# Decoder trunk on one core: the constants' table and two small tiles padded to multiples of 64 bytes

## The chip, the cores and the metric

The kernel runs on one core of a Trainium2 chip. The metric is the device time of one execution in microseconds; the kernel before is given as the median of three runs.

## The reference

A decoder trunk of two layers on 256 tokens of width 2048, all float32. Layer 0 mixes tokens with a Mamba-2 SSD mixer, layer 1 with forgetting attention (FoX):

```python
for i in range(DEPTH):
    hn = rmsnorm(h, norm_mix_pre[i])
    mix = ssd_mixer(hn, ...) if i % 2 == 0 else fox_mixer(hn, ...)
    h = h + rmsnorm(mix, norm_mix_post[i])
    ff = swiglu(rmsnorm(h, norm_ffn_pre[i]), ffn_w_gate[i], ffn_w_up[i], ffn_w_down[i])
    h = h + rmsnorm(ff, norm_ffn_post[i])
    pe = rmsnorm(p[i] @ ple_w_proj[i], ple_norm[i])
    h = h + jax.nn.sigmoid(h @ ple_w_gate[i]) * pe
```

Nearly all of the arithmetic is in the weight products: `ssd_in`, `ssd_out`, `fox_in`, `fox_out`, and for each layer gate, up (2048 to 5632), down (5632 to 2048), the gate of the per-layer input and its small projection. Their weights are some 500 MB, and each is read once.

## The kernel before

**Units and stages.** Activations lie with features on the partitions and the 256 tokens along the row. A weight product is cut into *units* of 2 to 6 blocks of 128 output features (`unit`, L196). A unit walks through its weights in *stages* of at most 1024 columns: `emit_stage` loads a stage from memory into a tile `raw`, ACT casts it to `wh` (L173, the part that fits fp32r), and DVE subtracts to get the rest, `wl` (L175). Activations are kept in the same two parts side by side: a tile of 512 columns, `x[:, 0, :]` high and `x[:, 1, :]` low. For each block and each 128 input features TensorE then runs a *pair*: a 512-column matmul of both parts against `wh` (L232) and a 256-column one of the high part against `wl` (L234). The weights are the stationary operand (each matmul has its own weight load) and the activations the moving one.

Two kinds of units differ. The last unit of some products (`sep`) runs three matmuls of 256 columns (L227 to L229) instead of a pair. The five token-major units of FoX (`tok`, L221 to L223) make the activations stationary and stream 412 or 416 columns of `wh` or `wl`.

**Which activations are in which tile.** `x`: ssd_in, the front half of ssd_out, gate, up, fox_out and the per-layer gate (5008 pairs, 384 `sep` matmuls). `xq`: the back half of ssd_out. `a`: the input of down. `xb`: the input of FoX. `psp`: the two tiles of the small projection, whose matmuls (L371 to L375, 256 columns each, same weight tiles) fill the time around a norm.

**Who decides the places.** Tiles come from pools that are laid one after another in each partition's memory, each tile at the next multiple of 32 bytes. The first pool, `cp`, begins with `vec`, a table of per-feature constants of `_NV` = 466 columns of 4 bytes, 1864 bytes. Everything up to the last tile of that pool, then the pools of weights, `h`, `x` and `ev`, follow behind it. `ev` holds `ms` and `rs`, the two-column statistics that `rstd_small` makes for a norm, 8 bytes each in slots of 32. The pools behind `ev` that hold `a`, `xq` and `xb` follow its end. The pool of `psp` is laid from the other end of the memory.

The built programs of before and of the change give these byte addresses within a partition (all buffers of a name share the remainder):

| Tile | First address before | mod 64 | mod 128 | First address after | mod 64 | mod 128 |
|---|---|---|---|---|---|---|
| wh | 43552 | 32 | 32 | 43584 | 0 | 64 |
| wl | 59936 | 32 | 32 | 59968 | 0 | 64 |
| x | 92704 | 32 | 32 | 92736 | 0 | 64 |
| a, xq, xb | 137920 | 0 | 64 | 138112 | 0 | 0 |
| psp | 225248 | 32 | 96 | 225248 | 32 | 96 |

Pieces inside a tile (a block of 128 weights is 512 bytes, half an activation tile 1024) keep these remainders. In the token-major units the second piece of a stage lies 1648 (412 columns) or 1664 bytes (416) behind the first.

Of the kernel before, what the change touches and what calls it, by code (L numbers as in the profile page):

```python
# [14 lines left out]
P = 128  # L15
# [29 lines left out]
_NV = 0  # L45
for _n, _w in (
# [4 lines left out]
    ("dt_bias", 1), ("a_log", 1),  # L51
):
    _VEC[_n] = _NV
    _NV += _w


def tile_trunk(ctx, tc, a, out):
# [17 lines left out]
    def nm(s):  # L75
        cnt[0] += 1
        return f"{s}_{cnt[0]}"
# [169 lines left out]
    def tmp(tag, shape=(P, T), dt=F32, bufs=2):  # L247
        return ev.tile(list(shape), dt, tag=tag, name=nm(tag), bufs=bufs)

    def misc():  # L250
        return psm.tile([P, 512], F32, tag="mi", name=nm("mi"))
# [24 lines left out]
    def rstd_small(acc, n):  # L276
        ps = misc()
        for j in range(2):
            PE.matmul(ps[:, j * P:(j + 1) * P], lhsT=acc[:, j * P:(j + 1) * P], rhs=ones,
                      start=True, stop=True)  # L280
        ms = tmp("ms", (P, 2))
        for j in range(2):
            dmark[0] = V.tensor_scalar(out=ms[:, j:j + 1], in0=ps[:, j * P:j * P + 1], scalar1=1.0 / n,  # L283
                                       scalar2=EPS, op0=mult, op1=add)
        rs = tmp("rs", (P, 2), bufs=3)
        G.tensor_tensor(out=rs, in0=ms, in1=mhalf, op=ALU.pow)  # L286
        return rs

# [91 lines left out]
    def post_norm(fill):  # L380
        for f in fill[:FILL_A]:
            f()
        rs = rstd_small(ssb, D)
        for _ in range(PRE_A):
            emit_stage(mark[0], dmark[0])
        for f in fill[FILL_A:FILL_B]:
            f()
        rstd_wide(rs, rwide)
        for _ in range(PRE_B):
            emit_stage(mark[0], dmark[0])  # L390
        for f in fill[FILL_B:]:
            f()
# [39 lines left out]
    def mk_r(half=True, small=None):  # L432
        r = []

        def f1():
            r.append(rstd_small(ssb, D))
            if small is not None:
                V.tensor_copy(out=small, in_=r[0])

        def f2():  # L440
            rstd_wide(r[0], rwide)
            if half:
                V.tensor_scalar(out=rwide2, in0=rwide, scalar1=0.5, scalar2=None, op0=mult)
        return f1, f2
# [19 lines left out]
    def tail(i, mpx, m, pp, mk_next):  # L464
# [63 lines left out]
        def mkpe():  # L528
            rs = rstd_small(ssp, D)
            rstd_wide(rs, rpe)  # L530
            V.tensor_scalar(out=rpe, in0=rpe, scalar1=0.5, scalar2=None, op0=mult)
# [561 lines left out]
```

## Time and profile before

| | |
|---|---|
| Median of three runs | 2813.49 us (2811.70 to 2813.92) |
| Span of the profiled execution, first to last instruction | 2811.0 us |
| TensorE busy | 2782.5 us, 99% of the span |
| VectorE (DVE) busy | 1927.1 us, 69% |
| ScalarE (ACT) busy | 1484.4 us, 53% |

The profiled execution has no time of its own beside its span; the span stands 2.5 us under the median of the three runs. In the rows below, a group of TensorE instructions is named by its line and tiles: `acc<-x,wh` is a matmul that writes `acc` with activations from `x` and weights from `wh`. Matmuls overlap, so the duration of one (some 0.39 us for 512 columns) is longer than the distance from its start to the next one's start; what a matmul costs in a full pipeline is that distance.

### The profile page before, as it was taken

How to read it: one execution, taken by the hardware profiler on the slowest of the kernel's cores; microseconds unless marked ns; L12 is line 12 of the kernel's file. 1: busy time of each engine (PE TensorE's matmuls, PEld its weight loads, DVE VectorE, ACT ScalarE, POOL GpSimd, SP SyncE). 2: the span in 40 equal slices, each digit the busy share in tenths (PEclk: the TensorE clock that was granted, in tenths of full speed). 3: DMA queues.
4: the chain of work that ended last, by engine and by line, in shares of the span. 5: the costliest groups of instructions: out<-in, count | busy, mean ns of one | idle time of the engine just before them, and what ended most of it. 6: DMA issues, size and time to landing. Idle time of an engine off the chain costs nothing.

```text
span 2811.0 us, 43190 instructions
## 1 busy us (share of the span) xinstructions
PE 2782.5 (99%) x16306; PEld 2439.5 (87%) x16306; DVE 1927.1 (69%) x3033; ACT 1484.4 (53%) x2455; POOL 182.8 (7%) x235
## 2 busy tenths in 40 slices
PE   9999999999999999999999999999999999999999
PEld 8888888889788888888897998888888888888888
DVE  8888888855966645666669556766866545666577
ACT  6586676544654444445446544555654444445454
POOL 2000000000300000000005000000200000000022
PEclk9999999999999999999999999999999999999999
DMA  7666665565566656666555676645666656656545
GB/s 234 189 196 184 190 191 173 159 201 180 158 201 188 188 192 189 187 177 192 195 169 166 184 209 191 177 161 164 180 189 188 194 188 185 192 171 204 193 153 176
DMA packets 262512, 520.09 MB, mean 185 GB/s; under 512 B 17392, under 2 KB 42128, under 8 KB 262304
## 3 DMA queue, kind: packets, MB, share of 16 engines
q1 hardware_dynamic: 258640, 504.96, 58.5%
q0 software_dynamic: 3520, 12.15, 1.4%
q8 instruction: 127, 2.08, 0.3%
q14 instruction: 81, 0.66, 0.1%
q10 hardware_dynamic: 144, 0.24, 0.0%
HBM read 515.10 MB, written 2.18 MB: 184 GB/s over the span
## 4 chain that ended last, share of the span: by engine, by line
PE 91%; DVE 4%; issue 3%; ACT 1%; POOL 0%; DMA 0%; DVEq 0%; ACTq 0%; POOLq 0%
PE acc L232 53%; PE acc L234 27%; PE acc L229 1%; PE acc L227 1%; PE acc L228 1%; PE acc L222 1%; PE acc L223 1%; PE acc L221 1%; DVE x L264 1%; PE mi L748 1%; DVE wl L175 1%; DVE sg L411 1%; ACT wh L173 0%; DVE x L261 0%; DVE h L419 0%
## 5 line engine op out<-in xcount | busy, mean ns | idle before, releaser
L232 PE MATMUL acc<-x,wh 128*128 128x512 f32 x5008 | 1730.7, 398 | 12.5 <-DVE x L264 6.7
L175 DVE TENSOR_TENSOR wl<-raw,wh 128x1024 fp32r<-128x1024 f32 (+4 forms) x1020 | 1182.9, 1165 | 793.4 <-ACT wh L173 790.4
L173 ACT CAST wh<-raw 128x1024 fp32r<-128x1024 f32 (+4 forms) x1020 | 1006.4, 993 | 1003.0 <-PE acc L232 825.2
L234 PE MATMUL acc<-x,wl 128*128 128x256 f32 x5008 | 1331.8, 281 | 7.0 <-DVE wl L175 6.8
L232 PEld LDWEIGHTS acc<-x,wh 128*128 128x128 f32 x5008 | 928.1, 188 | 226.0 <-DVE x L264 14.5
L234 PEld LDWEIGHTS acc<-x,wl 128*128 128x128 f32 x5008 | 932.1, 189 | 32.9 <-DVE wl L175 10.5
L232 PE MATMUL acc<-a,wh 128*128 128x512 f32 x1232 | 425.2, 392 | 0.0
L234 PE MATMUL acc<-a,wl 128*128 128x256 f32 x1232 | 339.2, 280 | 0.0
L232 PEld LDWEIGHTS acc<-a,wh 128*128 128x128 f32 x1232 | 229.9, 188 | 49.1
L234 PEld LDWEIGHTS acc<-a,wl 128*128 128x128 f32 x1232 | 231.4, 188 | 2.2
L232 PE MATMUL acc<-xb,wh 128*128 128x512 f32 x512 | 181.9, 398 | 0.0
L255 ACT COPY tb<-acc 128x256 f32<-128x256 f32 (+1 forms) x401 | 139.2, 369 | 38.5 <-PE acc L234 19.6
L234 PE MATMUL acc<-xb,wl 128*128 128x256 f32 x512 | 144.8, 283 | 0.0
L286 POOL TENSOR_TENSOR rs<-ms,mhalf 128x2 f32<-128x2 f32 x18 | 21.2, 1177 | 1764.5 <-DVE ms L283 1764.5
L232 PEld LDWEIGHTS acc<-xb,wh 128*128 128x128 f32 x512 | 95.9, 188 | 20.0
L234 PEld LDWEIGHTS acc<-xb,wl 128*128 128x128 f32 x512 | 96.4, 188 | 0.8 <-issue 0.2
L256 DVE TENSOR_TENSOR g<-acc,tb 128x256 f32<-128x256 f32 x204 | 78.6, 415 | 2.1 <-ACT tb L255 1.5
L232 PE MATMUL acc<-xq,wh 128*128 128x512 f32 x224 | 77.6, 392 | 0.0
L730 ACT ACTIVATE E<-ab,bias 128x128 f32<-128x128 f32 x192 | 59.7, 390 | 15.7 <-PE mi L750 14.8
L658 DVE SCALAR_TENSOR_TENSOR g<-xr,vec,g 128x256 f32<-128x256 f32 x144 | 62.5, 477 | 4.2 <-ACT g L655 3.8
L234 PE MATMUL acc<-xq,wl 128*128 128x256 f32 x224 | 62.3, 280 | 0.0
L273 POOL TENSOR_TENSOR ssb<-ssb,sqp 128x256 f32<-128x256 f32 x60 | 55.6, 927 | 61.9 <-ACT sqp L272 57.5
(209 smaller groups left out, 2305.9 us busy)
## 6 DMA issues: line engine op xcount, KB each, us to landing
raw<-down SPq DMA_DIRECT2D x176, 512.0 KB, 4.1
raw<-ssd_in SPq DMA_DIRECT2D x152, 512.0 KB, 4.6
raw<-gate SPq DMA_DIRECT2D x128, 512.0 KB, 4.3
raw<-up SPq DMA_DIRECT2D x128, 512.0 KB, 4.5
raw<-fox_in SPq DMA_DIRECT2D x64, 512.0 KB, 4.0
raw<-gate SPq DMA_DIRECT2D x64, 384.0 KB, 3.4
raw<-up SPq DMA_DIRECT2D x64, 384.0 KB, 3.7
raw<-ssd_out SPq DMA_DIRECT2D x40, 512.0 KB, 3.7
```

The lines of the kernel that those rows point to most:

```text
L173: A.copy(out=wh[:, :kc * n], in_=raw[:, :kc * n])
L175: V.tensor_tensor(out=wl[:, :kc * n], in0=raw[:, :kc * n], in1=wh.bitcast(F32)[:, :kc * n], op=sub)
L221: PE.matmul(o, lhsT=xh, rhs=wh[:, c, :], start=st, stop=False)
L222: PE.matmul(o, lhsT=xh, rhs=wl[:, c, :], start=False, stop=False)
L223: PE.matmul(o, lhsT=x[:, 1, t * P:(t + 1) * P], rhs=wh[:, c, :], start=False, stop=sp)
L232: PE.matmul(accs[t], lhsT=wh[:, c, t * P:(t + 1) * P], rhs=x.rearrange("p a n -> p (a n)"), start=st, stop=False)
L234: PE.matmul(accs[t][:, :T], lhsT=wl[:, c, t * P:(t + 1) * P], rhs=x[:, 0, :], start=False, stop=sp)
L255: A.copy(out=tb[:np_], in_=acc[:np_, T:2 * T])
L256: V.tensor_tensor(out=o, in0=acc[:np_, :T], in1=tb[:np_], op=add)
L273: (eng or V).tensor_tensor(out=acc, in0=acc, in1=sq, op=add)
L658: V.scalar_tensor_tensor(out=c, in0=xr[:, k:k + T], scalar=col(f"conv_w{k}", cc), in1=c, op0=mult, op1=add)
L730: A.activation(E[:, i, b * P:(b + 1) * P], ab[:, i, lo:lo + P], AF.Relu, scale=-1.0, bias=bias3[:, b, h0 + i:h0 + i + 1])
```

## The change

`_NV` is rounded up to a multiple of 16 columns, from 466 to 480 (1920 bytes), so all that lies behind `vec` moves by 32 bytes. `ms` and `rs` get 16 columns instead of 2, of which the first two are used, so their five slots take 64 bytes each instead of 32, and what lies behind them moves by 192 bytes in all. Every engine has the same instructions in the same order as before; the one that differs in size is the load of `vec`, 480 columns instead of 466.

```diff
@@ -52,6 +52,7 @@
 ):
     _VEC[_n] = _NV
     _NV += _w
+_NV = -(-_NV // 16) * 16
...
@@ -278,11 +279,11 @@
...
-        ms = tmp("ms", (P, 2))
+        ms = tmp("ms", (P, 16))[:, :2]
...
-        rs = tmp("rs", (P, 2), bufs=3)
+        rs = tmp("rs", (P, 16), bufs=3)[:, :2]
```

## Rows read from the trace of the kernel before

**Rows 1.** Page, parts 1 and 2: busy time of engines; granted TensorE clock by slice.

```profile
PE 2782.5 (99%) x16306; PEld 2439.5 (87%) x16306; DVE 1927.1 (69%) x3033; ACT 1484.4 (53%) x2455; POOL 182.8 (7%) x235
...
PEclk9999999999999999999999999999999999999999
```

**Rows 2.** Page, part 4: the chain that ended last, by engine.

```profile
PE 91%; DVE 4%; issue 3%; ACT 1%; POOL 0%; DMA 0%; DVEq 0%; ACTq 0%; POOLq 0%
```

**Rows 3.** Whole run, TensorE groups with shapes: count | busy us, mean ns | idle before.

```profile
L232 PE MATMUL acc<-x,wh 128*128 128x512 f32 x5008 | 1730.7, 398 | 12.5 <-DVE x L264 6.7 <-DVE x L261 2.4 <-ACT wh L173 0.8
L234 PE MATMUL acc<-x,wl 128*128 128x256 f32 x5008 | 1331.8, 281 | 7.0 <-DVE wl L175 6.8
L232 PE MATMUL acc<-a,wh 128*128 128x512 f32 x1232 | 425.2, 392 | 0.0
L234 PE MATMUL acc<-a,wl 128*128 128x256 f32 x1232 | 339.2, 280 | 0.0
...
L232 PE MATMUL acc<-xq,wh 128*128 128x512 f32 x224 | 77.6, 392 | 0.0
L234 PE MATMUL acc<-xq,wl 128*128 128x256 f32 x224 | 62.3, 280 | 0.0
...
L228 PE MATMUL acc<-a,wh 128*128 128x256 f32 x176 | 49.1, 280 | 0.0
...
L227 PE MATMUL acc<-x,wh 128*128 128x256 f32 x128 | 36.2, 283 | 0.0
...
L374 PE MATMUL acc<-psp,wh 128*128 128x256 f32 x64 | 17.8, 278 | 0.0
```

**Rows 4.** Timeline of TensorE, a stretch of units on x: start us, duration us.

```profile
881.09 0.39 PE L232 MATMUL acc<-x,wh 128*128 128x512 f32 x1
881.32 0.27 PE L234 MATMUL acc<-x,wl 128*128 128x256 f32 x1
...
897.73 0.39 PE L232 MATMUL acc<-x,wh 128*128 128x512 f32 x1
```

**Rows 5.** Timeline of TensorE, a later stretch of units on x.

```profile
903.33 0.40 PE L232 MATMUL acc<-x,wh 128*128 128x512 f32 x1
...
911.81 0.40 PE L232 MATMUL acc<-x,wh 128*128 128x512 f32 x1
```

**Rows 6.** Timeline of TensorE, a stretch of units on a.

```profile
1004.93 0.39 PE L232 MATMUL acc<-a,wh 128*128 128x512 f32 x1
...
1021.57 0.39 PE L232 MATMUL acc<-a,wh 128*128 128x512 f32 x1
```

**Rows 7.** Timeline of TensorE, a stretch of units on xb.

```profile
1683.26 0.39 PE L232 MATMUL acc<-xb,wh 128*128 128x512 f32 x1
...
1693.66 0.39 PE L232 MATMUL acc<-xb,wh 128*128 128x512 f32 x1
```

**Rows 8.** Timeline of TensorE, the filler matmuls on psp.

```profile
707.42 0.28 PE L371 MATMUL acc<-psp,wh 128*128 128x256 f32 x1
...
709.12 0.28 PE L371 MATMUL acc<-psp,wh 128*128 128x256 f32 x1
```

**Rows 9.** TensorE groups from 1085 to 1326 us (gate and up units alone).

```profile
L232 PE MATMUL acc<-x,wh 128*128 128x512 f32 x689 | 235.2, 395 | 0.0
L234 PE MATMUL acc<-x,wl 128*128 128x256 f32 x688 | 182.8, 279 | 0.0
```

**Rows 10.** Whole run, TensorE groups of the token-major units, 416 columns wide.

```profile
L223 PE MATMUL acc<-wh,xb 128*128 128x416 f32 x32 | 11.3, 352 | 0.0
L221 PE MATMUL acc<-wh,xb 128*128 128x416 f32 x32 | 11.3, 352 | 0.0
L222 PE MATMUL acc<-wl,xb 128*128 128x416 f32 x32 | 11.2, 349 | 0.0
```

**Rows 11.** Page, part 5: the weight split on DVE and ACT.

```profile
L175 DVE TENSOR_TENSOR wl<-raw,wh 128x1024 fp32r<-128x1024 f32 (+4 forms) x1020 | 1182.9, 1165 | 793.4 <-ACT wh L173 790.4
L173 ACT CAST wh<-raw 128x1024 fp32r<-128x1024 f32 (+4 forms) x1020 | 1006.4, 993 | 1003.0 <-PE acc L232 825.2
```

## The prediction

> **What bounds the kernel now.** I read the page's busy times first: TensorE is busy 99% of the span, and its clock is granted in full, 2.4 GHz, in every slice [rows 1]. The chain that ended last says the same: 91% of it is TensorE [rows 2]. So the question is not who waits but how far apart TensorE's instructions start. The engines that make the weights ready are no second limit. A stage of 1024 columns is eight pairs, some 2.8 us of TensorE; DVE takes 1.17 us for it and ACT 0.99, and DVE stood idle 793 us before this work and ACT 1003 us, ACT mostly until TensorE had freed a buffer [rows 11]. If pairs get a per cent faster, these two follow.
>
> Next, the distance from start to start. In a stretch of units on `a`, 48 pairs lie between the first row and the last: 16.64 us, 346.7 ns a pair [rows 6]. On `xb` 30 pairs take 10.40 us, again 346.7 [rows 7]. On `x` there are two rhythms: in one stretch 48 pairs take 16.64 us, 346.7 each [rows 4]; in a later one 24 pairs take 8.48 us, 353.3 each [rows 5]. The columns alone would take (512 + 256) / 2.4 = 320 ns, so a pair pays 27 or 33 ns on top. The same shapes, the same weight tiles, the same clock; what differs is the activation tile. By the table of places `x` begins 32 bytes past a multiple of 64 (all sixteen buffers), and `a`, `xq` and `xb` on one.
>
> The groups give means. The trace's durations overlap, but a constant ties them to the distances: on `a` the two durations add up to 392 + 280 = 672 ns [rows 3] against a distance of 346.7, so 162.7 ns each. Over the whole run `x` has 398 + 281 = 679 ns, 7 more than `a`; `xq`, aligned like `a`, has its 672 [rows 3]. Part of the 7 are waits: 12.5 + 7.0 = 19.5 us stand as idle before these groups [rows 3], 3.9 ns per pair. The rest is 3.1 ns, between the two rhythms. From 1085 to 1326 us, without any wait, `x` has 395 + 279 = 674, 2 more than `a` [rows 9]. In the three-matmul units a 256-column matmul has 283 ns on `x` and 280 on `a` [rows 3].
>
> **The change part by part.** No instruction is added, removed or moved. The wider load of `vec` is 14 columns more of 466 in one early transfer, and the padding of `ms` and `rs` costs only memory: I take both at nothing: the load is 7 KB more beside some 500 MB of weights that take the whole 2811 us, which uncovered would be 0.04 us.
>
> *Pairs on x.* Their activations come to a multiple of 64, where `a`, `xq` and `xb` lie today without ever showing the slower rhythm in rows 6 and 7. I take the price that leaves out the waits: 3.1 ns x 5008 = 15.5 us off the path. Bounds: 2 ns (the clean stretch, rows 9) gives 10 us; 7 ns (all of the difference, waits included) gives 35 us; nothing at all is a rival below.
>
> *Three-matmul units on x.* 283 to 280 ns, 3 ns x 384 = 1.2 us, bounds 0 and, at the same price for those on `a` and `xq` too, 3 us.
>
> *Token-major units.* Here the weights stream. With 412 columns the first of a stage's two pieces goes from 32 to 0 mod 64, the second from 16 to 48; with 416 both go from 32 to 0. At 3 ns, as above, the pieces that reach 0 (192 + 96 matmuls) give 0.9 us; the others I leave. Bounds: 0 and 1.4 us, or as much lost should 48 be worse than 16.
>
> *The weights as stationary operand.* All blocks of `wh` and `wl` go from 32 to 0 mod 64, for some 15,000 matmuls. No unit of today has both operands aligned, so this needs two ends. The token-major units hold aligned stationary tiles (`xb`, 0 mod 64) under misaligned moving ones: (352 + 352 + 349) / 3 = 351 ns [rows 10], less 162.7 is 188.3, 15 ns over 416 / 2.4 = 173.3. A 512-column matmul on `a`, with misaligned weights, has 392 - 162.7 - 213.3 = 16 ns over, a 256-column one 10.6. Aligned weights buy nothing visible there: end one, 0 us. The other end is the fastest matmul of the trace: the filler on `psp` starts 15 matmuls in 1.70 us, 113.3 ns each [rows 8], 4 ns under the 280 - 162.7 = 117.3 of `a`. If aligned weights brought every matmul there, 15,000 x 4 ns = 60 us. I take 0, since the filler's own weights are misaligned today and can't owe their speed to this.
>
> *Sum.* 15.5 + 1.2 + 0.9 = 17.6 us. The profiled span is 2811.0 us, so 2793.4; the span is 2.5 us under the median of the runs, so the forecast is 2796 us. What the pairs save is not taken back by the 19.5 us of waits on DVE and ACT unless all of those scale, and a per cent of 19.5 us is 0.2. The likeliest case's own range is 2790 to 2803.
>
> **The rivals.**
>
> *The place isn't what sorts the tiles: no change, 2811 to 2815 us.* `x` also lies lower in memory than `a`, `xq` and `xb`, and `x` stays where it is but for 32 bytes. For it: in part of its stretches `x` runs at 346.7 ns, misaligned as it is [rows 4], and `psp`, at 32 mod 64 too, has the fastest matmuls of all [rows 8]. Against it: in a stretch of 48 pairs twelve of the sixteen tiles, over 24 KB, take their turn without a change of rhythm [rows 4], and `a`, `xq` and `xb` agree with each other across both layers [rows 3, 6, 7].
> The Trainium skill gives this rival a reason: "SBUF — State Buffer", in its section "Door 1: The DMA port swizzle", puts the memory's lines at 16 bytes, so a tile at a multiple of 32 already begins on a line, and by that rule the padding buys nothing and the time stays at 2813. Rows 4 and 5 against rows 6 show a difference that this line size doesn't explain.
>
> *Aligned weights pay as well: 2736 to 2796 us*, the term above between its ends, 2766 in the middle. For it: every matmul still pays 10 to 16 ns over its columns, and the filler shows that 6.6 is possible. Against it: the token-major rows.
>
> *What counts is the distance between moving and stationary operand, mod 128: 2795 to 2804 us, but from other units.* The distances today are 0 for `x`, 32 for `a`, 64 for `psp`, and the 256-column matmuls take 120.3, 117.3 and 113.3 ns in that order. After the change `x` keeps 0 and `a`, `xq`, `xb` get 64. At the filler's best, 4 ns x (2 x 1968 + 624) = 18 us; at its mean of 278 ns [rows 3], 2 ns, 9 us.
>
> *Slower: equal remainders mod 64 collide.* If what makes `x` slow is that its blocks and those of `wh` sit at the same remainder, `x` stays slow (0 and 0) and the 1968 pairs on `a`, `xq` and `xb` join it: 3.1 ns x 1968 + 3 ns x 624 = 8 us, at the slow rhythm throughout 6.6 x 1968 + 1.9 = 15 us; 2821 to 2828. It decides from 2.9 ns a pair on, 0.2% of the run. Against it: `psp` and `wh` share 32 today and are fastest; the token-major units don't share, and pay 15 ns.
> By the Trainium skill, "TensorE: Matmul & The Clock Gate", the part "Step-by-step: what each phase is for", the moving operand and the weight load have read ports of their own and don't take from each other, so neither of these last two should exist. No row here shows the ports.
>
> **How the numbers follow.** Likeliest case 0.47; weights too 0.18; distance mod 128 0.12; no change 0.14; slower 0.09. Within 0.2% (5.6 us) of before is about what this measurement can't tell from no change. Faster: 0.47 + 0.18 + 0.12 = 0.77, of which I move 0.01 to the same for the weakest of the third. The range 2765 to 2815 holds the likeliest case, the distance case, no change, and half of the weights' case: 0.47 + 0.12 + 0.14 + 0.09 = 0.82.
>
> **What the profile after would show.** Right: `acc<-x,wh` and `acc<-x,wl` together at 672 to 676 ns in the whole-run groups, no stretch of `x` at 353 ns a pair, `acc<-a` unchanged at 392 and 280, the three-matmul units on `x` at 280. If the weights matter, `acc<-a` falls below 392 and 280 too. If it is the distance, `a` falls and `x` stays at 398 and 281. If remainders collide, `a` rises to `x`. If `x` and `a` both stay, the place wasn't it. The forecast fails most simply if aligned `x` has its own second rhythm.

## The result, and the profile after

The changed kernel takes 2818.99 us (median of ten runs, 2818.04 to 2820.79) against 2812.61 for the kernel before (ten runs, 2811.70 to 2813.92): the ratio is 1.0024 [1.0014, 1.0033], slower by 6.4 us and outside the predicted range. The interval lies wholly above 1, though it reaches down past the 0.2% that was named as the limit. The profiled execution spans 2817.1 us, 6.1 more than before.

In the page after (busy us, share, count; granted clock by slice; chain by engine) what has grown is TensorE's time, by 6.5 us (its weight loads, which overlap with it, by 2.3, and POOL, busy for 7% of the span, by 2.1): VectorE and ScalarE are within 1 us of before [rows 1, 2], and the clock is full.

```profile
PE 2789.0 (99%) x16306; PEld 2441.8 (87%) x16306; DVE 1926.4 (68%) x3033; ACT 1485.2 (53%) x2455; POOL 184.9 (7%) x235
...
PEclk9999999999999999999999999999999999999999
...
PE 90%; DVE 4%; issue 4%; ACT 1%; DMA 1%; POOL 0%; DVEq 0%; ACTq 0%; POOLq 0%
```

The TensorE groups of the whole run after (count | busy us, mean ns | idle before; line numbers are one higher than before):

```profile
L233 PE MATMUL acc<-x,wh 128*128 128x512 f32 x5008 | 1729.4, 398 | 12.4 <-DVE x L265 6.2 <-DVE x L262 2.6 <-ACT wh L174 1.0
L235 PE MATMUL acc<-x,wl 128*128 128x256 f32 x5008 | 1331.5, 281 | 6.7 <-DVE wl L176 6.6
L233 PE MATMUL acc<-a,wh 128*128 128x512 f32 x1232 | 429.8, 394 | 0.0
L235 PE MATMUL acc<-a,wl 128*128 128x256 f32 x1232 | 340.9, 281 | 0.0
L233 PE MATMUL acc<-xb,wh 128*128 128x512 f32 x512 | 184.4, 401 | 0.0
L235 PE MATMUL acc<-xb,wl 128*128 128x256 f32 x512 | 145.8, 285 | 0.0
L233 PE MATMUL acc<-xq,wh 128*128 128x512 f32 x224 | 78.4, 394 | 0.0
L235 PE MATMUL acc<-xq,wl 128*128 128x256 f32 x224 | 62.6, 281 | 0.0
...
L228 PE MATMUL acc<-x,wh 128*128 128x256 f32 x128 | 36.2, 283 | 0.0
...
L375 PE MATMUL acc<-psp,wh 128*128 128x256 f32 x64 | 17.9, 280 | 0.0
```

The group of `xb` in the same view of before:

```profile
L232 PE MATMUL acc<-xb,wh 128*128 128x512 f32 x512 | 181.9, 398 | 0.0
L234 PE MATMUL acc<-xb,wl 128*128 128x256 f32 x512 | 144.8, 283 | 0.0
```

Set beside [rows 3]: `x`, the group that should have gained, has the same 398, 281 and 283 ns. `a` and `xq`, which should have stayed, went from 392 and 280 to 394 and 281, `xb` from 398 and 283 to 401 and 285, and `psp` from 278 to 280. The stretch of gate and up units alone says the same of `x`, 395 and 279 ns as in [rows 9] (TensorE groups, 1085 to 1326 us, after):

```profile
L233 PE MATMUL acc<-x,wh 128*128 128x512 f32 x684 | 233.4, 395 | 0.0
L235 PE MATMUL acc<-x,wl 128*128 128x256 f32 x684 | 181.7, 279 | 0.0
```

And a stretch of units on `a` now shows the rhythm that only `x` had. TensorE's timeline after (start us, duration us):

```profile
1007.11 0.39 PE L233 MATMUL acc<-a,wh 128*128 128x512 f32 x1
...
1023.71 0.40 PE L233 MATMUL acc<-a,wh 128*128 128x512 f32 x1
```

47 pairs lie between the two rows: 16.60 us, 353.2 ns each, where [rows 6] gave 346.7. Not every stretch on `a` is that slow: over the whole run its pairs now average 350.7 ns.

To see where all of the time went I took from each trace every matmul's start to the next one's start, less its columns / 2.4, called that the "excess", and summed it by tile, where both matmuls belong to the six groups below; what is more than 40 ns over counts as a wait. The columns take 2421.0 us, all other matmuls and gaps about 111 us and waits at the other tiles some 7 us in the two kernels and in the variants tabled below, so these sums are what differs:

```
excess in us    x      a      xb     xq    token-major  psp   waits at x   first to last matmul
before        151.5   38.7   13.0   7.0      8.4        1.6      45.9           2805.7
after         150.6   43.6   15.4   7.8      7.4        1.9      45.8           2811.8
```

`a` +4.9, `xb` +2.4, `xq` +0.8, `psp` +0.3, `x` -0.9, token-major -1.0: +6.5 us against 6.1 measured. The loss is found, and nearly all of it is in the tiles that the prediction left alone.

### The profile page after: what moved, and what is told of

It is laid out like the page before. It is cut to its first block, busy times and chain, and to the rows that moved or that the text cites. A ratio compares the mean times of both kernels' runs of the same rounds, so it can differ in the third digit from the quotient of the medians.

```text
span 2817.1 us, 43190 instructions
## 1 busy us (share of the span) xinstructions
PE 2789.0 (99%) x16306; PEld 2441.8 (87%) x16306; DVE 1926.4 (68%) x3033; ACT 1485.2 (53%) x2455; POOL 184.9 (7%) x235
## 4 chain that ended last, share of the span: by engine, by line
PE 90%; DVE 4%; issue 4%; ACT 1%; DMA 1%; POOL 0%; DVEq 0%; ACTq 0%; POOLq 0%
PE acc L233 53%; PE acc L235 27%; PE acc L229 1%; PE acc L228 1%; PE acc L230 1%; PE acc L224 1%; PE acc L223 1%; PE acc L222 1%; DVE wl L176 1%; DVE x L265 1%; PE mi L749 1%; DVE sg L412 1%; DVE x L262 0%; DVE h L420 0%; ACT wh L174 0%
## 5 line engine op out<-in xcount | busy, mean ns | idle before, releaser
L235 PEld LDWEIGHTS acc<-x,wl 128*128 128x128 f32 x5008 | 931.6, 189 | 33.0 <-DVE wl L176 10.7
```

The source lines that it names most:

```text
L235: PE.matmul(accs[t][:, :T], lhsT=wl[:, c, t * P:(t + 1) * P], rhs=x[:, 0, :], start=False, stop=sp)
```

## The experiments

What the addresses suggested after the result: not where a tile lies counts, but how far the activations lie from the weights that TensorE holds. Taken modulo 256 bytes (activation address less weight address, from the built programs), `x` was at 0 and stays at 0, since table padding moves both; `a`, `xq` and `xb` went from 160 to 64, since 160 bytes of padded statistics tiles lie between them and the weights; `psp` went from 192 to 160. The main rival was the prediction's own, that equal remainders mod 64 collide.

**The two halves of the change.** One kernel has only the wider table, one only the wider statistics tiles.

```diff
 # table alone
+_NV += 14
 # statistics tiles alone
-        ms = tmp("ms", (P, 2))
+        ms = tmp("ms", (P, 16))[:, :2]
-        rs = tmp("rs", (P, 2), bufs=3)
+        rs = tmp("rs", (P, 16), bufs=3)[:, :2]
```

> Only the table is padded: weights, x and a all move by 32 bytes together, psp stays. Distance theory (what counts is the address of the moving tile minus that of the weights, mod 256): the distances stay 0 for x and 160 for a, xq and xb, so a stays at 346.7 ns a pair and the time at that of before, 2811 to 2815 us; only psp goes from 192 to 160 and its matmuls from about 113 to about 117 ns. Own-place theory (what counts is where a tile itself lies, and weights at a multiple of 64 cost): the weights are now at 64 mod 128, as in the change, so a goes to 349 to 353 ns a pair and the time to 2818 to 2821 us.

> Only the two statistics tiles are padded: a, xq and xb move by 160 bytes, weights and x stay. Distance theory: a, xq and xb are now 64 from the weights, as in the change, so a is at 349 to 353 ns a pair and the time at 2817 to 2821 us, the whole loss. Own-place theory with the weights as the cause: the weights have not moved, so 2811 to 2815 us. The rival of equal remainders mod 64 also expects the whole loss, since a and the weights both lie at 32 mod 64.

Table alone: 2812.58 us, ratio 1.0002 [0.9993, 1.0011]. Statistics tiles alone: 2819.03 us, 1.0025 [1.0015, 1.0034], all of the loss. Groups on `a` with the table alone:

```profile
L233 PE MATMUL acc<-a,wh 128*128 128x512 f32 x1232 | 425.2, 392 | 0.0
L235 PE MATMUL acc<-a,wl 128*128 128x256 f32 x1232 | 339.2, 280 | 0.0
```

and with the statistics tiles alone (line numbers as in the kernel before):

```profile
L232 PE MATMUL acc<-a,wh 128*128 128x512 f32 x1232 | 429.8, 394 | 0.0
L234 PE MATMUL acc<-a,wl 128*128 128x256 f32 x1232 | 340.9, 281 | 0.0
```

The first brings weights and `x` to multiples of 64 and takes `a` off them, and `a` keeps its 392 ns to the last tenth of a microsecond of busy time. In the second the weights and `x` stay at 32 past a multiple, `a` stays on one, and `a` slows. So a tile's own remainder doesn't decide it; the distance fits both, and so does the rival of equal remainders. By the distance `psp` was also to slow down with the table alone, from about 113 to 117 ns; its groups there went from 278 to 280, half of that.

**Other distances in the kernel.** Pads set the activation tiles apart from each other (`h` is the tile that lies ahead of `x`, `dg` one that lies ahead of `a`, `xq` and `xb`); the weights stay.

```diff
 # x at 192; a at 32 and 96 by layer, xq 128, xb 224
+    h = [hp.tile([P, T + (48 if c == NCH - 1 else 0)], F32, name=f"h{c}")[:, :T] for c in range(NCH)]
+        dg = tmp("dg", (P, T + 8), bufs=1)[:, :T]
+             pad(ap_, (40, 56)[i])
+        pad(p_, 24)
 # x at 96; a at 192 and 224, xq 192, xb 0: the same with 24, 48, (0, 8), 16
```

> Weights stay; distances mod 256 set to x 192, xq 128, a of layer 0 32, a of layer 1 96, xb 224. Distance theory: each of the five gets a rhythm of its own that need not be 346.7 or 353.3; x at 192, where psp showed 113 ns for 256 columns, goes below its mean of 350 ns a pair, to 333 to 347, and the time to 2740 to 2800 us. Equal remainders mod 64: x (still equal to the weights) stays at its mixture of 346.7 and 353.3, xq is slow at 350 to 353, and both a and xb, unequal, stay at 346.7: time 2811 to 2815 us.

> Weights stay; distances mod 256 set to x 96, xq and a of layer 0 192, a of layer 1 224, xb 0. Distance theory: xb at 0 shows the mixture of 346.7 and 353.3 ns a pair that x has today; a of layer 0 at 192 has the same rhythm as x of the other sweep, and a of layer 1 at 224 the same as xb there. Equal remainders mod 64: x, now unequal to the weights, stays at 346.7 throughout and the time falls by 15 to 20 us to some 2795 us; xq, a of layer 0 and xb, equal, are slow.

2825.39 us (1.0047 [1.0034, 1.0061]) and 2822.17 us (1.0035 [1.0021, 1.0049]): the hope that 192, where `psp` is fastest, would serve `x` fell. The first time lies outside both of its expected ranges, the second well above the 2795 us that equal remainders gave. In the first, in the stretch of gate and up units, `x` has 397 and 281 ns against 395 and 279:

```profile
L232 PE MATMUL acc<-x,wh 128*128 128x512 f32 x671 | 231.1, 397 | 0.0
L234 PE MATMUL acc<-x,wl 128*128 128x256 f32 x670 | 178.9, 281 | 0.0
```

The mean excess of a pair, from the starts, by distance over all kernels so far (and the next one, for `x` at 160):

```
distance   0          32     64            96          128    160            192          224
x         30.0                             30.4               27.2           32.8
a                    27.2    30.7          30.2               26.9           33.1         27.3
xb, xq    32.1               32.6, 30.3                31.1   27.4, 26.9          33.1    30.7
```

By equal remainders mod 64, distances 0, 64, 128 and 192 should be slow and 32, 96, 160, 224 fast. 96 is not fast, whether for `x` (30.4) or `a` (30.2); that rival falls as a mechanism. So does the distance modulo 128: 32 and 160 agree, but 96 and 224 on `a` do not (30.2, 27.3). Modulo 256 different tiles agree at 96 (30.4, 30.2), 160 (27.2, 26.9 to 27.4) and 192 (32.8 to 33.1), but two expectations of the second kernel missed: `xb` at 0 has 32.1 where `x` has 30.0, and `a` at 224 has 27.3 where `xb` has 30.7. The distance alone doesn't settle every place.

**x where a lies today.** `x` goes to 160, the others stay there.

```diff
-    h = [hp.tile([P, T], F32, name=f"h{c}") for c in range(NCH)]
+    h = [hp.tile([P, T + (40 if c == NCH - 1 else 0)], F32, name=f"h{c}")[:, :T] for c in range(NCH)]
-        dg = tmp("dg", bufs=1)
+        dg = tmp("dg", (P, T + 24), bufs=1)[:, :T]
```

> Weights stay; x, xq, a and xb all lie 160 bytes (mod 256) behind the weights, the distance that a, xq and xb have in the kernel before. Distance theory: x takes over their rhythm, 346.7 to 347 ns a pair without the slow one of 353.3, which is 3.1 ns x 5008 pairs and 2 ns x 384 three-matmul ones, 16 us: 2794 to 2798 us. If it was only coincidence that the sweeps shifted with the distance, x stays at its 350 and the time at 2811 to 2815 us.

2800.17 us (2799.83 to 2801.68) against 2812.70, ratio 0.9957 [0.9943, 0.9970]: it beats both kernels. Its groups, whole run:

```profile
L232 PE MATMUL acc<-x,wh 128*128 128x512 f32 x5008 | 1716.2, 394 | 14.6 <-DVE x L264 7.3 <-DVE x L261 3.7 <-ACT wh L173 1.1
L234 PE MATMUL acc<-x,wl 128*128 128x256 f32 x5008 | 1330.6, 281 | 8.4 <-DVE wl L175 8.4
...
L228 PE MATMUL acc<-x,wh 128*128 128x256 f32 x128 | 35.8, 280 | 0.0
```

and in the stretch of gate and up units, where nothing waits:

```profile
L232 PE MATMUL acc<-x,wh 128*128 128x512 f32 x688 | 233.2, 392 | 0.0
L234 PE MATMUL acc<-x,wl 128*128 128x256 f32 x690 | 183.4, 280 | 0.0
```

`x` has come to the 392 and 280 ns of `a`, its three-matmul units to 280. By the starts its excess fell from 151.5 to 137.0 us, 14.5, and the waits at `x` grew from 45.9 to 48.3: 12.1 net, against 12.5 by the medians. Of the 16 us expected, 1.5 didn't come in the excess, and 2.4 came back as those waits.

**TensorE alone.** This kernel leaves the whole trunk out: the same pair and three-matmul sequences on constant tiles, 32 pairs at each place of the activation in steps of 16 bytes, and then places of the weights. DVE, ACT and DMA are at 0 tenths in the page's slices, but for ACT in the first and DMA in the last. In outline:

```
for m in range(0, 128, 4):          # activation at 4 m bytes
    for k in range(8):
        for t in range(4):
            matmul(acc[t],         lhsT=w1[:, :128], rhs=mov[:, m:m + 512])
            matmul(acc[t][:, :256], lhsT=w2[:, :128], rhs=mov[:, m:m + 256])
```

> Leaves the whole trunk out: only TensorE works, on constant tiles, with pairs (512 columns, 256 columns) and with three matmuls of 256 columns, while the place of the moving tile goes up in steps of 16 bytes over 512 and that of the weights in steps of 32 over 256; the output is not the trunk's. Distance theory: the excess of a pair over 320 ns depends on the distance mod 256 alone, repeats after 256 bytes, and is the same whichever tile is moved: about 30 at 0, 27 at 32, 30 to 31 at 64, 96 and 128, 27 at 160, 33 at 192, 27 at 224. Something else in the trunk as the cause (writes of DVE, ACT or transfers into the same memory): the excess is the same at all places, near 27, since nothing else runs. It also says whether distances of an odd 16 bytes, which the trunk's tiles never have in pairs, are better, and whether the two weight tiles of a pair can be told apart.

Its timeline at distance 32, 24 pairs between the two rows, 8.32 us or 346.7 ns each:

```profile
41.71 0.39 PE L63 MATMUL acc<-mov,w 128*128 128x512 f32 x1
...
50.03 0.39 PE L63 MATMUL acc<-mov,w 128*128 128x512 f32 x1
```

and at distance 64, 8.48 us or 353.3 ns each:

```profile
64.07 0.40 PE L63 MATMUL acc<-mov,w 128*128 128x512 f32 x1
...
72.55 0.40 PE L63 MATMUL acc<-mov,w 128*128 128x512 f32 x1
```

So both rhythms of the trunk appear without any other engine, DMA or wait. Mean excess over 320 ns by distance; the second 256 bytes gave the first 256 again:

```
distance      0    16   32   48   64   80   96   112  128  144  160  176  192  208  224  240
pair         26.7 26.6 26.6 31.2 33.4 29.9 30.0 33.4 30.9 26.4 26.6 29.9 33.4 29.9 26.7 33.3
```

The trunk's order is there: 32, 160 and 224 low, 64 and 192 high, 96 and 128 between. Three places differ: 0 (26.7 here, 30.0 for `x` and 32.1 for `xb`), 64 (33.4 here, 30.3 to 32.6 in the trunk) and `xb` at 224 (30.7). When the weights were moved instead, two distances came out differently too: 224 at 33.6 and 64 at 28.9. So some places admit more than one rhythm. The three-matmul sequences of the same kernel have another order: 6.7 ns a matmul over its columns at 112 and 192, 10.7 at 160, 13.3 at 80 and 96. So 192, slow for pairs, is fast there, and the 113.3 ns of `psp` at 192 before, 6.6 over its columns, fit that; the three-matmul units on `x` don't, with 281 ns at 192 against 280 at 160. One pair of places, with the two weight tiles at different distances (192 for `w1`, 0 for `w2`), ran at 20.0 ns. That would be worth another 6.7 x 5008 = 34 us on `x`, and was looked for next.

**All combinations alone.** The same kernel (trunk left out) with the distances of the two weight tiles each in 16 steps, the 256 cells run in two orders; (192, 0) stands for 192 to `w1` and 0 to `w2`.

```
for d1 in range(0, 64, 4):          # then again with the loops exchanged and d2 downwards
    for d2 in range(0, 64, 4):
        pairs(0, d1, d2, 6)
```

> Leaves the trunk out again (constant tiles, TensorE alone, not the trunk's output): for pairs and for three matmuls, the distance of the moving tile to w1 (streamed against by the 512-column matmul) and to w2 goes independently over 16 steps of 16 bytes; the pairs are run twice in different orders, so that each follows another neighbour. Distance theory: the diagonal repeats the run before it (26.7, 26.6, 26.6, 31.2, 33.4 ... ns over 320), off the diagonal some places lie under 26.7, as 192 with 0 did (20 ns), and the two orders agree except where two rhythms exist. If 20 ns was an accident of the phase, the second order gives some 27 to 33 there.

The pairs stand on levels, the lowest 20.0, then some 23 to 24.5, 26.6, a band from 28 to 32, and 33.4 ns with a few up to 35, but 47 of the 256 cells differ by more than 1.5 ns between the orders: (192, 0) 33.2 in one and 20.0 in the other, (64, 0) 30.0 and 20.0, (0, 0) 33.6 in both and 26.7 in the kernel ahead. (192, 112) and (64, 240) gave 20 in both, and equal distances of 32 or of 160 gave 26.6 to 26.8 in both. The expectation that equal distances repeat the table above held, to within 0.7 ns, at seven of the sixteen (32, 64, 80, 96, 128, 160, 192); at the other nine at least one order missed it, by up to 7 ns. So the table is that of one order of running. What ran ahead can set which rhythm a place takes; at 32 and 160 it didn't.

**The 20 ns rhythm in the trunk.** Three kernels set `wh` and `wl` apart from each other, all activations at one distance: (192, 0), (64, 240) and (192, 112).

```diff
 # 192 and 0: a tile of 48 columns between wh and wl; dg wider by 24 columns
+            G.memset(wp.tile([P, 48], F32, name="wpad"), 0.0)
 # 64 and 240; 192 and 112: wl begins 80 bytes into a wider tile; h wider by 16; by 48;
 # in both dg wider by 24 columns, and dtv in a buffer of dg
+        wl = wp.tile([P, SW + 64], F32R, tag="wl", name=f"wl{i}", bufs=WB)[:, 20:20 + SW]
```

> The whole trunk with the two weight tiles told apart: x, xq, a and xb lie 192 bytes (mod 256) from wh and 0 from wl. Distance theory, from the matmuls alone: 340 ns a pair against 350 on x and 346.8 on a, xq and xb: 10 ns x 5008 + 6.8 ns x 1968, some 60 us less, 2745 to 2765 us, the three-matmul units (1008 matmuls) and the token-major ones unknown to 4 ns each. If the 20 ns over 320 was an accident of the phase, the pairs stay between 346 and 354 and the time between 2795 and 2830 us.

> x, xq, a and xb lie 64 bytes (mod 256) from wh and 240 from wl, one of the two places where the matmuls alone ran at 20 ns over 320 in both orders. If the rhythm of 340 ns a pair holds in the trunk: 10 ns x 5008 + 6.8 ns x 1968, 63 us less, near 2750 us. If the units' ends and the small matmuls between them throw it out of that rhythm, as where 192 and 0 gave 28 ns in the mean, the pairs mix 20 with 27 and 33 and the time is 2770 to 2815 us.

> The other such place: 192 bytes from wh and 112 from wl. Same two outcomes: near 2750 us if the rhythm of 340 ns a pair holds in the trunk, 2770 to 2815 us if it mixes with others.

2808.43 us (0.9986 [0.9977, 0.9996]), 2823.88 us (1.0043 [1.0029, 1.0056]) and 2814.61 us (1.0007 [0.9998, 1.0016]). The first gains a little, the second loses, the third gives no change. In the first, pairs on `x` average 28.5 ns over: a fifth of them stand at 20 to 22, nearly all others between 28 and 37. In the second again a fifth stand at 20, but two thirds at 33 or 34, and its time lies above both of the ranges expected; in the third 12% stand at 20 to 22. The 20 ns rhythm occurs in the trunk but does not hold there. All three lose to `x` at 160. Why it doesn't hold was not found.

**The change with only the distance put back.** The changed kernel, all its padding kept, plus 96 bytes ahead of `a`, `xq` and `xb`, which puts them at 160 again.

```diff
-        dg = tmp("dg", bufs=1)
+        dg = tmp("dg", (P, T + 24), bufs=1)[:, :T]
```

> The changed kernel, with only one more pad of 96 bytes ahead of a, xq and xb, so that they are at 160 bytes from the weights again (and no longer at multiples of 64); table, statistics tiles, weights and x stay padded. Distance theory: the whole loss goes, 2811 to 2814 us. Something else in the change as the cause (the weights at a multiple of 64, the padded statistics tiles): the time stays at 2817 to 2821 us.

2812.82 us against 2812.12, ratio 1.0002 [0.9993, 1.0011]: the loss is gone. Groups on `a`:

```profile
L233 PE MATMUL acc<-a,wh 128*128 128x512 f32 x1232 | 425.2, 392 | 0.0
L235 PE MATMUL acc<-a,wl 128*128 128x256 f32 x1232 | 339.2, 280 | 0.0
```

By the starts, the excess of `a`, `xb` and `xq` is 38.7, 12.9 and 7.0 us again, as before the change (38.7, 13.0, 7.0). The same sums for four of the variants above, beside those of before and after:

```
excess in us       x      a      xb     xq    token-major  psp   waits at x   first to last matmul
x at 160         137.0   38.7   13.0   7.0      8.4        1.6      48.3           2793.2
x at 192         161.4   41.5   14.7   8.2      7.1        1.5      45.1           2818.9
x at 96          154.2   43.3   15.2   8.5      7.5        1.7      45.4           2815.4
change, a at 160 150.7   38.7   12.9   7.0      8.4        2.0      47.0           2806.0
```

## Why the prediction was wrong, step by step

- **The step that failed** is "Pairs on x": "Their activations come to a multiple of 64, where `a`, `xq` and `xb` lie today without ever showing the slower rhythm". The remainder mod 64 was only one of the things that told `x` from `a`; another was the distance to the weights, 0 against 160, and that was the cause: with the table alone `x` lies on a multiple of 64 and keeps 283 ns and 30 ns of excess a pair, and at 160 it has the 392 and 280 ns of `a`. The change left `x`'s distance as it was, so 15.5 us of expected gain became 0.9 by the starts. The size itself was right for the move that the kernel did not make: `x` at 160 gave 14.5 us.
- **"`a` unchanged at 392 and 280"** failed with it. The padding between the weights and `a` was seen, but only its remainder was looked at. It cost 4.9 + 2.4 + 0.8 us. The rival of equal remainders gave 2821 to 2828 for `a` joining `x`'s slow rhythm, the right sign and, by luck, close in size; its mechanism is refuted by distance 96. The rival of the distance had the right quantity and the wrong period: mod 128 it put `a` at `psp`'s place and forecast a gain; mod 256 `a` went to 64 and `psp` had been at 192, and in pairs both are slow places.
- **Three-matmul units:** 1.2 us expected on `x`, none came, 283 ns before and after. At 160 they fell to 280, as the term had it.
- **Token-major units:** 0.9 us expected, 1.0 measured in the sum of starts. It comes from the statistics tiles too: with the table alone the sum stayed at 8.4 us, with the statistics tiles alone it fell to 7.4. The reason given, pieces that reach a multiple of 64, is therefore wrong: the table alone brings them there. That the size came out is luck.
- **The weights' own place, 0 us:** right. The table alone aligned both weight tiles for 15,000 matmuls and gave 1.0002.
- **The bound:** right. TensorE's starts set the time: 6.5 us of excess became 6.1 of span, and for `x` at 160 the 14.5 us were passed on but for 2.4 that came back as waits, more than the 0.2 us allowed for.
- **The two rules of the Trainium skill.** Of "SBUF — State Buffer", "Door 1: The DMA port swizzle", the prediction drew that tiles on 16-byte lines gain nothing from padding to 64 and the time would stay at 2813. For alignment as such the table alone agrees (2812.6), but the whole change measured 2819.0, and steps of whole 16-byte lines moved the excess of a pair between 26.4 and 33.4 ns. From "TensorE: Matmul & The Clock Gate", "Step-by-step: what each phase is for", with ports of their own for the moving and stationary operands, no effect of their relative place was to be expected; the measurement decides against that consequence, by 14.5 us on `x`. What inside the memory or TensorE makes it so, no run shows.

**What stays open.** The table by distance is measured, not explained. At distances such as 0, 64 and 224 more than one rhythm is possible, and what sets it, beyond that the instructions ahead matter, was not found; that is also why the 20 ns rhythm could not be held.

## What to carry to other kernels

Two tiles that differ in speed usually differ in more than one way; before crediting an alignment, list what else about their places differs, above all the distance between the two operands of a matmul, and vary one of them alone: one half of this change, run by itself, shows that a tile's own alignment isn't it. A padding moves everything laid behind it, so its effect is read from the addresses of the built program, tile by tile, and not from the tile that is padded. For pairs like these, measure the distance from start to start at a few relative places and put the tile with the most matmuls at a good one: `x` at 160 for 256 bytes of padding in all gives 2800 us.

## What was not expected of the hardware

- The spacing of these fp32r matmuls depends on the activations' address relative to the weights': by up to 7 ns a pair in the run of TensorE alone, in steps as small as 16 bytes. There a shift of 256 bytes, run in the same order, gave the same table again; in the trunk `a` keeps its 38.7 us of excess in the kernel with `x` at 160, where it lies 256 bytes further from the weights than before.
- Over whole stretches the mean is often 346.7 or 353.3 ns a pair, and 340.0 in a few places of the runs alone; others lie between. Both 346.7 and 353.3 appear with every other engine idle, so they need no contention with them.
- The same place can hold two rhythms, by what ran ahead: (192, 0) gave 353.2 and 340.0 ns in two orders.
- The best distance depends on the sequence: with TensorE alone 192 gave 33.4 ns of excess in a pair, the most, and 6.7 ns a matmul, the least, in the three-matmul sequences.
